# Four subtractions that move behind a normalisation in VectorE's queue

## The chip, the cores and the metric

The kernel runs on one core of a Trainium2 chip. The metric is the device time of one execution in microseconds. Before the change three runs gave 1221.09, 1221.14 and 1221.6 us; the median is 1221.14.

The engines are named as in the profile: PE is TensorE, PEld its weight loads, DVE is VectorE, ACT is ScalarE, POOL is GpSimd, SP is the engine that issues most transfers. L177 is line 177 of the kernel.

## The reference

The program computes two layers of a decoder trunk on 256 tokens of width 1024, in float32. Each layer is

```
x = LN(alpha*x + 0.5*SwiGLU_1(x))
x = LN(alpha*x + Mixer(x))
x = LN(alpha*x + 0.5*SwiGLU_2(x))

def _layernorm(x, g, b):
    mu = mean(x);  var = mean((x - mu)**2)
    return (x - mu) * rsqrt(var + 1e-5) * g + b

def _swiglu(x, w1, w3, w2):
    return (silu(x @ w1) * (x @ w3)) @ w2        # 1024 -> 2816 -> 1024
```

The mixer begins with one projection of x and holds a gated position mixing, a differential attention over 8 heads and an output projection. It matters here only in that its first product needs the normalised x, as the first product of a feed-forward block does.

## The kernel before, in words

**Products in three parts.** Every float32 operand is split into a high part (a copy of type fp32r, which the matmuls take) and a low part, what the copy lost. A product is the sum of three matmuls, high by high, high by low, low by high (`three`, L255). So each weight matrix that comes from memory takes three steps: a load of 1 MB into one of four buffers (`raw`), a copy by ScalarE into `whi` (L173), and a subtraction by VectorE that gives `wlo` (L177). The buffer is free for another load once both have read it. `stream` does this for one load. Its argument `after` names an instruction behind which the subtractions are put in VectorE's queue; an empty one means `latest[1]`, the last low part of the input's own split.

**Tokens and order.** The 256 tokens are two tiles of 128. TensorE's order is that of the program text, with side work put between the products by a list of tasks that count TensorE's progress (`beat`, `beside`). On the other engines a scheduler sets the order, bound by the data and by `behind(ins)`, which ties what is traced inside it behind `ins` on the same engine.

**The norm.** A feed-forward block ends with the class `Norm`. For each token tile, `finish_s` forms the mean, has ScalarE sum the squares (L536), computes the reciprocal root by a chain of small VectorE instructions (`rsqrt`, L227 to L233, 128x1 each), and normalises the rows in two halves of 512 columns (L539). The second of these two instructions is kept as `ends[t]`. Then each half is turned: four transposes by TensorE into a side bank (L608), gain and offset by ScalarE (L614), and a split into high (L217) and low (L218) part. `xlo[t, h]` keeps the low part's instruction of half h of tile t. The turned rows are what the next product reads; `self.x[0]` holds the first half's columns, `self.x[1]` the second's.

**The next product.** Behind a feed-forward norm the next matrix is multiplied by `gemm_b2`: for the first token tile, c = 0 and 1 (halves of the depth), m = 0 and 1 (halves of the width); then the same for the second tile. Four loads serve it. The first two are prepared inside the block before (`ahead`, `rest_of`; then `norm.pre` is set), the third and the fourth by `stream` at c = 1. The fourth load (n = 3, c = 1, m = 1) is the last stream that the change speaks of; `after[3]` is its tie. TensorE multiplies the first tile with the first three loads and turns the two halves of the second tile in between: the first half after six of the twelve matmuls of the third load, the second half after six of the twelve of the fourth.

There are three such places in a run: the first feed-forward norm of either layer (next is the mixer's value projection, `in_wb`) and the second feed-forward norm of the first layer (next is `in_w13b` of the second layer). Behind the mixer's norms `norm.pre` is not set.

Of the kernel before, what the change touches and what calls it, by code (L numbers as in the profile page):

```python
# [57 lines left out]
def trunk(ctx, tc, x, xT, w13a, w13b, w2s, w2p, wb, wqk, wa, wbr, wo, gateb, sgug, sgub, sguwT, sgubias, lam, diffg,  # L58
# [22 lines left out]
    def bank():  # L81
        return psum.tile([P, 512], F32, tag="main", name=name("bank"))
# [67 lines left out]
    def behind(ins):  # L150

        return tc.issue_after(ins) if ins is not None else nullcontext()

    def stream(src, width=CH, sub=HC, lent=(), after=(None, None)):

        step()
        raw = raw_pool.tile([P, CH], F32, tag="raw", name=name("raw"))
        nc.sync.dma_start(raw[:, :width], src)  # L160
        out = []
        for o in range(0, width, HC):
            if o // HC in lent:
                hi, lo = ([act.tile([P, 512], F32R, tag="slot", name=name(n)) for _ in range(2)] for n in ("lhi", "llo"))
                at = [(hi[j], lo[j]) for j in range(2)]
            else:
                hi = hi_pool.tile([P, HC], F32R, tag="hi", name=name("whi"))
                lo = lo_pool.tile([P, HC], F32R, tag="lo", name=name("wlo"))
                at = [(hi[:, p : p + sub], lo[:, p : p + sub]) for p in range(0, HC, sub)]
            for p, (h, w) in zip(range(0, HC, sub), at):  # L170
                r = raw[:, o + p : o + p + sub]
                with behind(latest[0] if o // HC in lent else early[0] or latest[0]):
                    copied = A.activation(h, r, AF.Copy)  # L173
                if o // HC in lent:
                    early[0] = copied.ins
                with behind(after[o // HC] or latest[1]):
                    V.tensor_tensor(out=w, in0=r, in1=h.bitcast(F32), op=ALU.subtract)  # L177
            out.append((hi, lo))
        return out
# [22 lines left out]
    def rest_of(pre, after):  # L202

        (_, hi0, lo0), (raw, hi1, lo1) = pre
        lows(pre[1], after)
        hi = hi_pool.tile([P, HC], F32R, tag="hi", name=name("whi"))
        lo = lo_pool.tile([P, HC], F32R, tag="lo", name=name("wlo"))
        for p in range(0, HC, 512):
            r, h, w = (v[:, o + p : o + p + 512] for v, o in ((raw, HC), (hi, 0), (lo, 0)))
            with behind(early[0]):  # L210
                A.activation(h, r, AF.Copy)
            with behind(after):
                V.tensor_tensor(out=w, in0=r, in1=h.bitcast(F32), op=ALU.subtract)
        return [(hi0[:2], lo0[:2]), (hi0[2:], lo0[2:])], [(hi1, lo1), (hi, lo)]
# [71 lines left out]
    def rows_b(ps, t, k0, piece, xh, xl, kts, c0=0, n=512):  # L286

        hi, lo = piece
        for j in range(2):
            k, o = k0 + j, j * 512 + c0  # L290
            wh, wl = (w[j][:, c0 : c0 + n] if isinstance(w, list) else w[:, o : o + n] for w in (hi, lo))
            three(ps[:, :n], xh(k)[:, t * P : (t + 1) * P], xl(k)[:, t * P : (t + 1) * P], wh, wl,
                  k == 0, k == kts - 1)
        beat(n / 1024)
# [66 lines left out]
    def gemm_b2(srcs, xh, xl, done, norm=None):  # L361

        lent, after = [()] * 4, [(None, None)] * 4
        if norm:
            lent = [(0, 1), (0,), (), ()]
            after[1:3] = [(norm.ends[0], norm.ends[0])] * 2
        ps = [[bank() for _ in range(2)] for _ in range(NT)]
        got = [[None] * 4 for _ in range(2)]  # L370
        for t in range(NT):
            for c in range(2):
                if norm:
                    norm.ready(t, c)
                    after[3] = [norm.xlo.get((0, 1))] * 2
                for m in range(2):
                    n = 2 * c + m
                    if t == 0 and n < 2 and norm and norm.pre:
                        if n == 0:
                            got[0][:2], got[1][:2] = rest_of(norm.pre, norm.ends[0])  # L380
                    elif t == 0:
                        got[m][2 * c : 2 * c + 2] = stream(srcs[m][:, c * CH : (c + 1) * CH], sub=512, lent=lent[n],
                                                           after=after[n])
                    for i in range(2 * c, 2 * c + 2):
                        rows_b(ps[t][m], t, 2 * i, got[m][i], xh, xl, KT)
            early[0] = None
            with behind(latest[0] if t == 0 else None):
                done(t, ps[t])
# [238 lines left out]
    def ffn(l, f, i, norm, following=None):  # L627
# [59 lines left out]
        if norm is None:  # L687
            gemm_first([w13b[l, f, 0, 0], w13b[l, f, 1, 0]], front(0))
        else:
            gemm_b2([w13b[l, f, 0, 0], w13b[l, f, 1, 0]], xh, xl, front(0), norm=norm)  # L690
# [65 lines left out]
    def mixer(l, i, norm):  # L756
# [6 lines left out]
        def got_val(t, ps):  # L763
            for h in range(2):
                A.activation(val[t][:, h], ps[h], AF.Copy)

        gemm_b2([wb[l, VAL_, 0], wb[l, VAL_, 1]], xh, xl, got_val, norm=norm)

        hb = slots("hb", 2 * KT, F32R)
# [200 lines left out]
        def done(t, ps):  # L970
            for h in range(2):
                ln.part(t, h * 512, ps[h])
            ln.finish(t, ((2, 1.5), (2, 1))[t])

        gemm_b2([wo[l, 0], wo[l, 1]], view(m_hi), view(m_lo), done)
        return ln.close()

    norm = None
    for l in range(DEPTH):
        norm = ffn(l, 0, 0, norm, [wb[l, 1, m] for m in range(2)])  # L980
        norm = mixer(l, 1, norm)
        norm = ffn(l, 1, 2, norm, [w13b[l + 1, 0, m, 0] for m in range(2)] if l < DEPTH - 1 else None)
# [92 lines left out]
```

## Time and profile before

| what | value |
|---|---|
| runs | 1221.09, 1221.14, 1221.6 us |
| profiled execution, its own time | 1220.97 us |
| its span | 1219.3 us |
| granted TensorE clock | 1.00 |
| PE busy | 1210.0 us (99%) |
| DVE busy | 948.8 us (78%) |
| ACT busy | 820.0 us (67%) |
| POOL busy | 87.7 us (7%) |
| L177, subtractions | 396 instructions, 437.8 us |
| L255 and its like, 128x512 matmul | 0.39 us each by the profile |
| read from memory | 235.47 MB |

Times inside the profile count from the start of the span. The matmuls are pipelined: each shows some 0.39 us, but the next starts 0.23 us after it. What TensorE loses is therefore read from start to start, and the idle time that the profile prints in brackets ahead of an instruction is somewhat less than the loss. A row of waits reads: engine and line that waited, what it waited for, microseconds in total, times, longest.

### The profile page before, as it was taken

How to read it: one execution, taken by the hardware profiler on the slowest of the kernel's cores; microseconds unless marked ns; L12 is line 12 of the kernel's file. 1: busy time of each engine (PE TensorE's matmuls, PEld its weight loads, DVE VectorE, ACT ScalarE, POOL GpSimd, SP SyncE). 2: the span in 40 equal slices, each digit the busy share in tenths (PEclk: the TensorE clock that was granted, in tenths of full speed). 3: DMA queues.
4: the chain of work that ended last, by engine and by line, in shares of the span. 5: the costliest groups of instructions: out<-in, count | busy, mean ns of one | idle time of the engine just before them, and what ended most of it. 6: DMA issues, size and time to landing. Idle time of an engine off the chain costs nothing.

```text
span 1219.3 us, 16603 instructions
## 1 busy us (share of the span) xinstructions
PE 1210.0 (99%) x6033; PEld 1018.2 (84%) x6033; DVE 948.8 (78%) x1540; ACT 820.0 (67%) x1340; POOL 87.7 (7%) x184
## 2 busy tenths in 40 slices
PE   9999999999999999999999999999999999999998
PEld 8888888888888888888878888888888888888886
DVE  6658998886587985579985679979856879747797
ACT  7677676689665575775766776666786655667761
POOL 0100000244100000000000000002430000000000
PEclk9999999999999999999999999999999999999999
DMA  8976666654644667665667655656546456576551
GB/s 319 334 246 178 218 226 214 214 169 165 249 171 167 216 176 264 192 202 210 218 218 252 194 176 205 255 215 202 165 175 232 173 172 243 177 238 209 181 202 48
DMA packets 82339, 252.29 MB, mean 207 GB/s; under 512 B 47520, under 2 KB 48592, under 8 KB 55632
## 3 DMA queue, kind: packets, MB, share of 16 engines
q1 hardware_dynamic: 78288, 238.31, 58.1%
q0 software_dynamic: 3536, 12.13, 3.1%
q8 instruction: 47, 0.77, 0.2%
q10 hardware_dynamic: 432, 0.79, 0.2%
q14 instruction: 36, 0.29, 0.1%
HBM read 235.47 MB, written 1.05 MB: 194 GB/s over the span
## 4 chain that ended last, share of the span: by engine, by line
PE 97%; DVE 1%; ACT 1%; DMA 0%; issue 0%; DVEq 0%; ACTq 0%
PE bank L255 36%; PE sbank L255 26%; PE bank L267 17%; PE bank L274 9%; PE sbank L267 2%; PE bank L430 2%; PE sbank L274 1%; PE sbank L805 1%; PE sbank L608 1%; DVE wlo L177 1%; PE sbank L854 1%; PE sbank L935 1%; ACT xf L614 0%; ACT sq L536 0%; PE sbank L852 0%; PE sbank L876 0%
## 5 line engine op out<-in xcount | busy, mean ns | idle before, releaser
L177 DVE TENSOR_TENSOR wlo<-raw,whi 128x1024 fp32r<-128x1024 f32 (+1 forms) x396 | 437.8, 1122 | 158.9 <-ACT whi L173 118.7
L173 ACT ACTIVATE whi<-raw 128x1024 fp32r<-128x1024 f32 (+1 forms) x396 | 375.5, 972 | 163.8 <-PE bank L255 61.7
L255 PE MATMUL bank<-whi,x 128*128 128x512 f32 x840 | 264.6, 390 | 0.0
L255 PEld LDWEIGHTS bank<-whi,x 128*128 128x128 f32 x840 | 157.7, 188 | 32.5
L255 PE MATMUL bank<-wlo,x 128*128 128x512 f32 x420 | 163.5, 389 | 0.0
L255 PE MATMUL sbank<-whi,x 128*128 128x512 f32 x512 | 159.0, 389 | 0.0
L267 PE MATMUL bank<-x,whi 128*128 128x512 f32 x640 | 158.3, 395 | 0.0
L267 PEld LDWEIGHTS bank<-x,whi 128*128 128x128 f32 x640 | 116.5, 188 | 25.9 <-issue 2.6
L255 PEld LDWEIGHTS sbank<-whi,x 128*128 128x128 f32 x512 | 96.1, 188 | 20.0
L337 ACT ACTIVATE shi<-raw 128x1024 fp32r<-128x1024 f32 (+1 forms) x80 | 73.4, 946 | 51.7 <-DVE raw L352 26.4
L255 PE MATMUL sbank<-wlo,x 128*128 128x512 f32 x256 | 99.6, 389 | 0.0
L339 DVE TENSOR_TENSOR slo<-raw,shi 128x1024 fp32r<-128x1024 f32 (+1 forms) x80 | 85.3, 1088 | 14.1 <-ACT shi L337 13.1
L255 PEld LDWEIGHTS bank<-wlo,x 128*128 128x128 f32 x420 | 78.9, 188 | 16.0
L274 PE MATMUL bank<-x,wlo 128*128 128x256 f32 x640 | 85.9, 285 | 0.0
L274 PEld LDWEIGHTS bank<-x,wlo 128*128 128x128 f32 x640 | 81.6, 191 | 2.3
L275 ACT ACTIVATE r<-bank 128x256 f32<-128x256 f32 x112 | 41.9, 379 | 27.6 <-PE bank L274 27.6
L614 ACT ACTIVATE xf<-sbank,ln_b,ln_g 128x128 f32<-128x128 f32 x80 | 30.0, 455 | 42.1 <-PE sbank L608 42.1
L255 PE MATMUL sbank<-whi,hhi 128*128 128x512 f32 x144 | 56.4, 391 | 0.0
L255 PEld LDWEIGHTS sbank<-wlo,x 128*128 128x128 f32 x256 | 48.0, 188 | 9.9
L255 PE MATMUL sbank<-wlo,hhi 128*128 128x512 f32 x144 | 56.1, 389 | 0.0
L255 PE MATMUL sbank<-whi,hlo 128*128 128x512 f32 x144 | 56.1, 389 | 0.0
L490 POOL DMA_DIRECT2D bc<-in_lng x6 | 3.2, 532 | 711.2 <-DVE bc L489 711.2
(246 smaller groups left out, 1984.6 us busy)
## 6 DMA issues: line engine op xcount, KB each, us to landing
raw<-in_w13b SPq DMA_DIRECT2D x76, 1024.0 KB, 5.3
raw<-in_w2p SPq DMA_DIRECT2D x24, 1024.0 KB, 4.8
raw<-in_wa SPq DMA_DIRECT2D x24, 1024.0 KB, 5.3
raw<-in_w2s SPq DMA_DIRECT2D x20, 1024.0 KB, 4.8
raw<-in_wb SPq DMA_DIRECT2D x16, 1024.0 KB, 5.2
raw<-in_wqk SPq DMA_DIRECT2D x16, 1024.0 KB, 5.0
raw<-in_wbr SPq DMA_DIRECT2D x16, 1024.0 KB, 4.8
raw<-in_w13a SPq DMA_DIRECT2D x8, 1024.0 KB, 4.8
```

Source lines behind the costliest of these rows:

```text
L173: copied = A.activation(h, r, AF.Copy)
L177: V.tensor_tensor(out=w, in0=r, in1=h.bitcast(F32), op=ALU.subtract)
L255: PE.matmul(ps, xx, w, start=start and n == 0, stop=stop and n == 2)
L267: PE.matmul(b[-1], hi[:, k * P : (k + 1) * P], xc(k), start=k == 0, stop=False)
L274: PE.matmul(b[n][:, :T], lo[:, k * P : (k + 1) * P], xc(k)[:, :T], start=False, stop=k == KT - 1)
L275: emptied[0] = A.activation(r[:, s], b[n][:, T:], AF.Copy, scale=scale).ins
L337: A.activation(h, r, AF.Copy)
L339: V.tensor_tensor(out=w, in0=r, in1=h.bitcast(F32), op=ALU.subtract)
L430: PE.matmul(ps[t][m], x[:, j, o + t * P : o + (t + 1) * P], y, start=k0 + j == 0 and o == 0 and y is hi, stop=k0 + j == KT - 1 and y is lo)
L608: PE.transpose(b[:, k * P : (k + 1) * P], self.y[t][:, h * 512 + k * P : h * 512 + (k + 1) * P], ident)
L614: A.activation(xf[:, s], b[:, s], AF.Identity, scale=self.gT[:, f], bias=self.bT[:, f])
L805: PE.matmul(banks[m][:, j * nk : (j + 1) * nk], rows(qT, m, j, t * P, P), rows(kT, m, j, 0, nk), start=True, stop=True)
```

## The change

One line of `gemm_b2` is changed. Where the input comes from a feed-forward norm, the fourth load's subtractions are tied behind `norm.ends[1]`, the second half of the second token tile's normalisation, instead of behind the low part of the first tile's second half. Behind a mixer norm the tie stays as it was.

```diff
             for c in range(2):
                 if norm:
                     norm.ready(t, c)
-                    after[3] = [norm.xlo.get((0, 1))] * 2
+                    after[3] = [norm.ends[1] if norm.pre else norm.xlo.get((0, 1))] * 2
                 for m in range(2):
```

No instruction is added or removed, and the order on PE, ACT, POOL and SP stays as it was. VectorE's order differs at the three places. The first of them, at the end of the first layer's first feed-forward block (xtok_144 is the second token tile, nwy and nwa are the links of its reciprocal root, wlo_1817 and wlo_1823 the low parts of the fourth load, x_1207 and x_1208 the turned rows); - is before, + is the change:

```order
 L218 TENSOR_TENSOR x_1208<-xf_1707,x_1208 128x4x128
 L233 TENSOR_SCALAR nwy_1725<-nwa_1724,yi_1721 128x1
-L177 TENSOR_TENSOR wlo_1817<-raw_1814,whi_1816 128x512
 L232 TENSOR_SCALAR nwa_1728<-nwy_1725,ve_1720 128x1
-L177 TENSOR_TENSOR wlo_1817<-raw_1814,whi_1816 128x512
 L233 TENSOR_SCALAR nwy_1729<-nwa_1728,nwy_1725 128x1
-L177 TENSOR_TENSOR wlo_1823<-raw_1814,whi_1822 128x512
 L232 TENSOR_SCALAR nwa_1732<-nwy_1729,ve_1720 128x1
-L177 TENSOR_TENSOR wlo_1823<-raw_1814,whi_1822 128x512
 L233 TENSOR_SCALAR nwy_1733<-nwa_1732,nwy_1729 128x1
 L539 TENSOR_SCALAR xtok_144<-xtok_144,mv_1715,nwy_1733 128x512 x2
+L177 TENSOR_TENSOR wlo_1817<-raw_1814,whi_1816 128x512 x2
+L177 TENSOR_TENSOR wlo_1823<-raw_1814,whi_1822 128x512 x2
```

The four subtractions stood one by one between the links of the root; now they stand together behind the two halves of the normalisation, ahead of the low parts of the second tile's turned rows (L218).

TensorE's order at the same place, which is the same before and after, shows who reads them. whi_1784 and wlo_1785 belong to the third load, sbank_1796 and sbank_1834 take the turned halves of the second tile:

```order
L608 MATMUL sbank_1796<-ident,xtok_144 128x128 [waits DMASW1_49,DVE_49]
L608 MATMUL sbank_1796<-ident,xtok_144 128x128 x3
L255 MATMUL bank_1740<-whi_1784,x_1208 128x512
L255 MATMUL bank_1740<-wlo_1785,x_1208 128x512
L255 MATMUL bank_1740<-whi_1784,x_1208 128x512 x2
L255 MATMUL bank_1740<-wlo_1785,x_1208 128x512
L255 MATMUL bank_1740<-whi_1784,x_1208 128x512
L255 MATMUL bank_1741<-whi_1816,x_1208 128x512
L255 MATMUL bank_1741<-wlo_1817,x_1208 128x512 [waits DVE_49]
L255 MATMUL bank_1741<-whi_1816,x_1208 128x512 x2
L255 MATMUL bank_1741<-wlo_1817,x_1208 128x512 [waits DVE_49]
L255 MATMUL bank_1741<-whi_1816,x_1208 128x512
```

These are the rows after the change. The rows stand where they stood; new are the waits for VectorE at the two matmuls that read wlo_1817, and in the same way at the two that read wlo_1823 behind the next transposes.

## The prediction

> **What bounds the kernel now.** First the head of the page, with the busy time of the engines and the shares of the chain of waits that ended last:
>
> ```profile
> span 1219.3 us, 16603 instructions
> PE 1210.0 (99%) x6033; PEld 1018.2 (84%) x6033; DVE 948.8 (78%) x1540; ACT 820.0 (67%) x1340; POOL 87.7 (7%) x184
> PE 97%; DVE 1%; ACT 1%; DMA 0%; issue 0%; DVEq 0%; ACTq 0%
> ```
>
> TensorE is busy 99% of the span and carries 97% of the chain. Nothing can be gained on another engine unless TensorE stands still for it. So the second view is the list of TensorE's waits; these four rows are all of it, and the row of the weight loads that belongs to the first stands below them:
>
> ```profile
> PE sbank L608 <- DVE xtok L539: 2.9, 3, 1.0
> PE sbank L442 <- DVE warm L438: 1.0, 1, 1.0
> PE sbank L576 <- DVE xtok L555: 1.0, 1, 1.0
> PE sbank L580 <- ACT minus L578: 0.2, 1, 0.2
> PEld sbank L608 <- DVE xtok L539: 4.2, 3, 1.4
> ```
>
> The transposes of the normalised rows (L608) wait three times for L539, the normalisation itself: 2.9 us by TensorE's row and 4.2 us by that of the weight loads. The others lie at the start and at the end of the program. The third view is TensorE's timeline around those three waits, and around a group of the same transposes that did not wait (177.64):
>
> ```profile
> 177.41 0.39 PE L255 MATMUL sbank<-whi,hlo 128*128 128x512 f32 x1
> 177.64 0.60 PE L608 MATMUL sbank<-ident,xtok 128*128 128x128 f32 x4
> 178.00 0.48 PE L255 MATMUL sbank<-whi,hhi 128*128 128x512 f32 x1
> ...
> 189.28 0.39 PE L255 MATMUL bank<-whi,x 128*128 128x512 f32 x1
> 190.65 0.66 PE L608 MATMUL sbank<-ident,xtok 128*128 128x128 f32 x4 [0.98 <-DVE xtok L539]
> 191.06 0.48 PE L255 MATMUL bank<-whi,x 128*128 128x512 f32 x1
> ...
> 614.05 0.39 PE L255 MATMUL bank<-whi,x 128*128 128x512 f32 x1
> 615.41 0.65 PE L608 MATMUL sbank<-ident,xtok 128*128 128x128 f32 x4 [0.97 <-DVE xtok L539]
> 615.82 0.48 PE L255 MATMUL bank<-whi,x 128*128 128x512 f32 x1
> ...
> 793.57 0.39 PE L255 MATMUL bank<-whi,x 128*128 128x512 f32 x1
> 794.93 0.66 PE L608 MATMUL sbank<-ident,xtok 128*128 128x128 f32 x4 [0.97 <-DVE xtok L539]
> 795.34 0.48 PE L255 MATMUL bank<-whi,x 128*128 128x512 f32 x1
> ```
>
> The durations overlap, so a stall is read from starts. Unhindered, the matmul after the transposes starts 178.00 - 177.41 = 0.59 us behind the matmul ahead of them. In the three waits it is 191.06 - 189.28 = 1.78, 615.82 - 614.05 = 1.77 and 795.34 - 793.57 = 1.77. The stalls are therefore 1.19, 1.18 and 1.18 us, together 3.55. Without a stall the transposes would start 0.23 us behind the matmul ahead of them (177.64 - 177.41), that is at 189.51 instead of 190.65.
>
> **What the change removes.** At each of the three places VectorE runs the rsqrt chain of the second token tile (L232 and L233 in turn on 128x1), then L539 in two halves. Four subtractions (L177, 128x512) stand between the chain's links. These are VectorE's rows at the first place, and then the same links for the first token tile, where nothing stands between them:
>
> ```profile
> 186.79 0.21 DVE L233 TENSOR_SCALAR nwy<-nwa,yi 128x1 f32<-128x1 f32 x1
> 186.91 0.68 DVE L177 TENSOR_TENSOR wlo<-raw,whi 128x512 fp32r<-128x512 f32 x1
> ...
> 189.20 0.68 DVE L177 TENSOR_TENSOR wlo<-raw,whi 128x512 fp32r<-128x512 f32 x1
> 189.80 0.21 DVE L233 TENSOR_SCALAR nwy<-nwa,nwy 128x1 f32<-128x1 f32 x1
> 190.04 1.00 DVE L539 TENSOR_SCALAR xtok<-xtok,mv,nwy 128x512 f32<-128x512 f32 x2
> ...
> 173.98 0.21 DVE L233 TENSOR_SCALAR nwy<-nwa,yi 128x1 f32<-128x1 f32 x1
> 175.35 1.01 DVE L539 TENSOR_SCALAR xtok<-xtok,mv,nwy 128x512 f32<-128x512 f32 x2
> 176.27 0.68 DVE L524 SCALAR_TENSOR_TENSOR xtok<-xtok,sbank 128x512 f32<-128x512 f32 x1
> 176.87 0.69 DVE L524 SCALAR_TENSOR_TENSOR xtok<-xtok,v 128x512 f32<-128x512 f32 x1
> ```
>
> From the first L233 to L539 it is 190.04 - 186.79 = 3.25 us with the subtractions, and 175.35 - 173.98 = 1.37 us without. The price of the bare chain is thus bounded by 1.37 and 3.25. I take 1.37: it is the same links on the same engine, 13 us earlier. The first L233 stays at 186.79, since all that stands ahead of it keeps its place. L539 then starts at 186.79 + 1.37 = 188.16 instead of 190.04. TensorE began 190.65 - 190.04 = 0.61 us after L539's start, which is the first half and the signal, so the transposes can run from 188.77. TensorE comes to them at 189.51. The data are 0.74 us early and the whole stall goes. The reserve also says how good the price must be: up to a chain of 1.37 + 0.74 = 2.11 us nothing of the gain is lost; beyond that each 0.1 us costs 0.1 us at each place. That the other two places are the same shows in VectorE's busy time (second number, with its instructions) from that first L233 to the end of L539's first half:
>
> ```profile
> 186.79:190.59 3.80, 3.76 (x12) 1.00 0.67 261
> 611.55:615.35 3.80, 3.76 (x12) 1.00 0.69 263
> 791.07:794.87 3.80, 3.76 (x12) 1.00 0.68 261
> ```
>
> **What it moves, and what is late next.** The four subtractions now stand behind L539. Behind L539 the next instruction starts 0.92 us after L539's start (176.27 - 175.35), and 128x512 instructions follow each other by 0.60 (176.87 - 176.27). So they start at 189.08, 189.68, 190.28 and 190.88 and end, 0.69 each, at 189.77 up to 191.57. Three things wait on them or behind them.
>
> First TensorE's matmuls, which today read the first and the last of the four at
>
> ```profile
> 192.74 0.39 PE L255 MATMUL bank<-wlo,x 128*128 128x512 f32 x1
> 195.25 0.39 PE L255 MATMUL bank<-wlo,x 128*128 128x512 f32 x1
> ```
>
> and, 1.19 earlier, at 191.55 and 194.06. The first subtraction is 1.78 us ahead of its reader, the last 2.49. Each of the two halves between them has as much within a few tenths. These matmuls get a wait of their own, which the wait for L539 covered until now; it is met long before, so I price it at nothing.
>
> Second, on VectorE's queue behind them, the low part of the second tile's turned rows (L218), which waits for ScalarE, and ScalarE for the transposes:
>
> ```profile
> 193.54 0.69 DVE L218 TENSOR_TENSOR x<-xf,x 128x512 fp32r<-128x512 f32 x1 [2.50 <-ACT x L217]
> 204.58 2.00 ACT L173 ACTIVATE whi<-raw 128x1024 fp32r<-128x1024 f32 x2
> ```
>
> Moved by 1.19 it can start at 192.35, and VectorE is free at 191.57. The 2.50 us of idle time ahead of it are the cover; without it, each tenth of a microsecond over would push L218, and no more. So the entire sequence of transposes, L614, L217 and L218 moves forward with TensorE.
>
> Third the input buffer. The last of the four subtractions is what frees it, and the queue of loads waits for that:
>
> ```profile
> 189.94 0.33 SPq L160 DMA_DIRECT2D raw<-in_wqk x1
> 203.12 2.60 SPq L160 DMA_DIRECT2D raw<-in_wqk  x2
> ...
> raw<-in_wqk SPq DMA_DIRECT2D x1, 1024.0 KB, 4.8
> ```
>
> Today the subtraction ends at 189.20 + 0.68 = 189.88 and the load goes out at 189.94. It will go out at about 191.57 + 0.06 = 191.63, 1.69 us later, and land at 196.43 instead of 194.74. Its data are the fourth 1 MB piece of the next stage; the ScalarE row above begins with the second half of the third piece, and the fourth follows as the second of that row's two at some 205.5, or 204.3 after the shift. That is a reserve of 7.9 us, and the next load goes out only at 203.12, when the next stage has freed a buffer. No instruction is added or taken away, so VectorE, ScalarE and the queues do the same work.
>
> **Sum.** The profiled execution took 1220.97 us, span 1219.3 plus 1.67 around it. 1220.97 - 1.19 - 1.18 - 1.18 = 1217.42. The median of the runs, 1221.14, lies 0.17 above the profiled execution (runs from 1221.09 to 1221.6), which gives 1217.59 from there; I say 1217.5. The size of the stall itself has bounds: 2.9 us by TensorE's idle time (which the overlapping durations make too small), 4.2 us by that of the weight loads, hence 1218.1 and 1216.8.
>
> **Rivals.**
>
> *The chain stays slow.* The bare chain takes more than 2.11 us, for instance because its links cost more while ScalarE reads the same rows. Halfway from 2.11 to today's 3.25 it keeps 0.57 us of the 1.14 us by which the transposes are late: about 1.7 of the 3.55 us are left, 1219.2. Against it: the links of the first tile took 1.37 with the same neighbours. Chance 0.05.
>
> *The gap is a shortage of buffers, or the gain is taken back further on.* The transposes would wait for a free side bank rather than for L539, or a later wait on something that does not shift would take up the 1.19; the time stays at 1221.0. The bank that the second tile's first transposes take was last read by VectorE in this row:
>
> ```profile
> 178.67 0.69 DVE L528 SCALAR_TENSOR_TENSOR xtok<-xtok,sbank 128x512 f32<-128x512 f32 x1
> ```
>
> It was free at 179.4, ten microseconds before it is wanted, and the four rows of TensorE's waits show no wait behind these places that could take something up. Chance 0.07. [...]
>
> *Slower.* The later release of the input buffer decides. If the fourth piece of the next stage set its pace, that stage would begin 1.69 us later than today at each place, the gain ahead of it would be lost, and the time would be 1220.97 + 3 x 1.69 = 1226.0. That begins where the load takes more than 4.8 + 7.9 = 12.7 us. For it speaks that the release is really put off; against it the 4.8 us of the load and the reserve. Chance 0.03.
>
> **How the numbers follow.** The forecast, all three stalls gone, has 0.85, and its own range is 1216.8 to 1218.3, from the bounds of the stall and the scatter of the runs. The range reaches to the slow chain's 1219.2; what it leaves out, no change, slower and the worse half of the slow chain, is about 0.13. A measurement of this kernel can tell about 0.2% from no change, that is 2.4 us, or 1218.7. Faster than that: the forecast and somewhat less than half of the slow chain, 0.87. Within 0.2%: 0.07 and the rest of the slow chain, 0.10. Slower: 0.03.
>
> **What would show it.** The changed kernel's list of TensorE's waits has no row L608 <- L539, and PEld's neither; the matmul behind the transposes starts 0.59 us after the one ahead of them at all three places; L539 follows the first L233 of its chain by about 1.4 us; four L177 follow it without a gap; L218 still waits for ScalarE. A row that has TensorE wait for wlo L177 would show the moved work late, one that has ScalarE wait for a load in the stage behind would show the buffer. The forecast is wrong if L539 comes more than 2.1 us behind that L233, or if the stall is gone and the span is not shorter by about 3.5.

## The result and the profile after

The changed kernel takes 1217.84 us (median of eight runs, 1217.45 to 1218.23); the kernel before, on the same chip, takes 1221.2 (eight runs, 1221.03 to 1221.96). That is 3.36 us less, a ratio of 0.9971 with a 95% interval of 0.996 to 0.9982 (0.29% less, 0.18% to 0.4%). The forecast was 1217.5, its range 1216.8 to 1219.2. The profiled execution took 1217.86 us, 3.11 less than the one before.

The head of the changed kernel's page, with the busy times and the shares of the chain of waits:

```profile
span 1216.2 us, 16603 instructions
PE 1209.8 (99%) x6033; PEld 1018.9 (84%) x6033; DVE 949.7 (78%) x1540; ACT 820.0 (67%) x1340; POOL 87.8 (7%) x184
PE 99%; DMA 0%; DVE 0%; ACT 0%; DVEq 0%; issue 0%; ACTq 0%
```

The busy times are those of before within 1 us. TensorE's share of the chain rose from 97% to 99%, and VectorE's went from 1% to 0. The list of TensorE's waits, all of it:

```profile
PE sbank L442 <- DVE warm L438: 1.0, 1, 1.0
PE sbank L576 <- DVE xtok L555: 1.0, 1, 1.0
PE sbank L580 <- ACT minus L578: 0.2, 1, 0.2
```

The row L608 <- L539 is gone, and no row has taken its place. TensorE's timeline at the three places (start, duration, instruction):

```profile
189.41 0.39 PE L255 MATMUL bank<-whi,x 128*128 128x512 f32 x1
189.64 0.60 PE L608 MATMUL sbank<-ident,xtok 128*128 128x128 f32 x4
189.99 0.49 PE L255 MATMUL bank<-whi,x 128*128 128x512 f32 x1
...
613.02 0.39 PE L255 MATMUL bank<-whi,x 128*128 128x512 f32 x1
613.26 0.60 PE L608 MATMUL sbank<-ident,xtok 128*128 128x128 f32 x4
613.61 0.48 PE L255 MATMUL bank<-whi,x 128*128 128x512 f32 x1
...
791.36 0.39 PE L255 MATMUL bank<-whi,x 128*128 128x512 f32 x1
791.59 0.60 PE L608 MATMUL sbank<-ident,xtok 128*128 128x128 f32 x4
791.94 0.49 PE L255 MATMUL bank<-whi,x 128*128 128x512 f32 x1
```

From the matmul ahead of the transposes to the one behind them it is now 0.58, 0.59 and 0.58 us, where it was 1.78, 1.77 and 1.77: 3.57 us less in all. VectorE at the first place:

```profile
186.91 0.21 DVE L233 TENSOR_SCALAR nwy<-nwa,yi 128x1 f32<-128x1 f32 x1
...
188.02 0.21 DVE L233 TENSOR_SCALAR nwy<-nwa,nwy 128x1 f32<-128x1 f32 x1
188.27 1.00 DVE L539 TENSOR_SCALAR xtok<-xtok,mv,nwy 128x512 f32<-128x512 f32 x2
189.19 2.49 DVE L177 TENSOR_TENSOR wlo<-raw,whi 128x512 fp32r<-128x512 f32 x4
192.48 0.69 DVE L218 TENSOR_TENSOR x<-xf,x 128x512 fp32r<-128x512 f32 x1 [0.80 <-ACT x L217]
```

The chain from the first L233 to L539 takes 188.27 - 186.91 = 1.36 us. This execution runs 0.13 us late from its first 8 us on, so the rows at this place stand 0.10 to 0.13 later than forecast. The four subtractions end at 189.19 + 2.49 = 191.68. Their first and last readers, then the load that waits for the last of them, and the ScalarE rows of the next stage:

```profile
191.70 0.40 PE L255 MATMUL bank<-wlo,x 128*128 128x512 f32 x1
...
194.24 0.39 PE L255 MATMUL bank<-wlo,x 128*128 128x512 f32 x1
```

```profile
191.75 0.33 SPq L160 DMA_DIRECT2D raw<-in_wqk  x1
...
203.56 2.00 ACT L173 ACTIVATE whi<-raw 128x1024 fp32r<-128x1024 f32 x2
```

The load goes out at 191.75 (forecast 191.63), and the ScalarE row, whose second instruction reads it from 204.51 on, has no idle time ahead of it. The moved work is late for nobody.

**Where a part of the gain went.** Laid side by side matmul by matmul, TensorE starts 0.13 us late and gains 3.50 us on the kernel before at the three places, so that it is 3.36 us ahead behind the third. It keeps this until 874 us. Then it loses 0.3 us in one group of the attention's score matmuls (L805), here in the kernel after and then in the kernel before:

```profile
874.85 1.42 PE L805 MATMUL sbank<-qk,qk 64*128 64x256 f32 x8
```

```profile
878.22 1.13 PE L805 MATMUL sbank<-qk,qk 64*128 64x256 f32 x8
```

The loss comes from 24 us earlier. VectorE scales probabilities (L832, L824) while GpSimd forms a product of the rotary embedding (L781). First VectorE's and GpSimd's timelines of the kernel after, then of the kernel before:

```profile
850.57 0.22 DVE L832 SCALAR_TENSOR_TENSOR c<-rc,neg_lam,sums 128x4 f32<-128x4 f32 x1
850.83 2.43 DVE L824 SCALAR_TENSOR_TENSOR pp<-pp,c,pp 128x256 f32<-128x256 f32 x4
850.96 1.49 POOL L781 TENSOR_TENSOR swap<-swap,sin_t 128x512 f32<-128x512 f32 x1 [4.78 <-DVE c L832]
```

```profile
853.92 0.96 DVE L832 SCALAR_TENSOR_TENSOR c<-rc,neg_lam,sums 128x4 f32<-128x4 f32 x1
854.92 1.41 DVE L824 SCALAR_TENSOR_TENSOR pp<-pp,c,pp 128x256 f32<-128x256 f32 x4
853.58 1.28 POOL L781 TENSOR_TENSOR swap<-swap,sin_t 128x512 f32<-128x512 f32 x1 [4.04 <-DMA swap<-z]
```

Before, L832 is held until about the end of L781 (it ends at 854.88, L781 at 854.86) and takes 0.96 us instead of 0.22. After, L781 begins a little later against VectorE, 0.39 us behind the start of L832 instead of 0.34 ahead of it, and one of the four L824 is held instead: it takes 1.50 us from 851.23 on, the one ahead of it 0.48. From the start of L832 to the end of the last L824 it is 2.41 us before and 2.69 after. Behind them VectorE's work is 3.07 us ahead of before, where it had been 3.36 ahead, and ten microseconds later ScalarE's is 3.08 ahead. TensorE, still 3.36 ahead, loses the difference when it reaches this L805; 0.26 of it remains to the end. So the profile's gain is 3.50 - 0.13 (start) - 0.26 = 3.11, and the spans differ by 3.1.

### The profile page after: what moved, and what is told of

It is laid out like the page before. It is cut to its first block, busy times and chain, and to the rows that moved or that the text cites. A ratio compares the mean times of both kernels' runs of the same rounds, so it can differ in the third digit from the quotient of the medians.

```text
span 1216.2 us, 16603 instructions
## 1 busy us (share of the span) xinstructions
PE 1209.8 (99%) x6033; PEld 1018.9 (84%) x6033; DVE 949.7 (78%) x1540; ACT 820.0 (67%) x1340; POOL 87.8 (7%) x184
## 3 DMA queue, kind: packets, MB, share of 16 engines
HBM read 235.47 MB, written 1.05 MB: 194 GB/s over the span
## 4 chain that ended last, share of the span: by engine, by line
PE 99%; DMA 0%; DVE 0%; ACT 0%; DVEq 0%; issue 0%; ACTq 0%
PE bank L255 38%; PE sbank L255 26%; PE bank L267 17%; PE bank L274 9%; PE sbank L267 2%; PE bank L430 2%; PE sbank L274 1%; PE sbank L805 1%; PE sbank L608 1%; PE sbank L854 1%; PE sbank L935 1%; PE sbank L852 0%; PE sbank L876 0%; PE sbank L839 0%; DMA xraw<-in_xT 0%; PE sbank L844 0%
## 5 line engine op out<-in xcount | busy, mean ns | idle before, releaser
L614 ACT ACTIVATE xf<-sbank,ln_b,ln_g 128x128 f32<-128x128 f32 x80 | 30.1, 457 | 38.6 <-PE sbank L608 38.6
```

Of the source, the lines that this page charges most:

```text
L614: A.activation(xf[:, s], b[:, s], AF.Identity, scale=self.gT[:, f], bias=self.bT[:, f])
```

## The experiments

**One place alone.** If the three stalls are independent and each is the order on VectorE, the tie at the first place alone takes a third of the gain, and nothing elsewhere.

```diff
-    after[3] = [norm.xlo.get((0, 1))] * 2
+    after[3] = [norm.ends[1] if norm.pre and norm.first else norm.xlo.get((0, 1))] * 2
...
-    self.ends, self.xlo, self.pre = [None] * NT, {}, None
+    self.ends, self.xlo, self.pre, self.first = [None] * NT, {}, None, (l, i) == (0, 0)
```

> The new tie at the first of the three places only (the first layer's first feed-forward norm); the other two as before. If the late normalisation alone makes the stall, the places are independent: TensorE has lost 1.1 to 1.2 us at the first place less than before and waits for L539 at the other two, 0.97 us of idle time each; about 1220.0 us. If a shortage of banks or buffers sets the gap, the first place keeps its gap and the time stays at 1221.2.

Measured: 1220.08 us (1219.8 to 1220.91; before 1221.25), ratio 0.9991, interval 0.9981 to 1.0. TensorE's list of waits has, of the row in question,

```profile
PE sbank L608 <- DVE xtok L539: 1.9, 2, 1.0
```

Two waits are left of three. Against the changed kernel TensorE falls back by 1.12 and 1.13 us at the other two places, and by less than 0.1 anywhere else. The places are independent, and a third of the change takes a third of the gain. A shortage of buffers or banks would not have yielded to the order at one place.

**Half the subtractions moved.** This puts the chain's length between the two known ones, near the break-even of 2.11 us. The tie holds only for the second of the load's two half-width pieces.

```diff
-    after[3] = [norm.xlo.get((0, 1))] * 2
+    after[3] = [norm.xlo.get((0, 1)), norm.ends[1] if norm.pre else norm.xlo.get((0, 1))]
```

> At all three places only two of the four subtractions stand behind the normalisation, the other two stay between the links of the chain. By the rows of the changed kernel the distance from the first L233 to L539 is then 1.36 plus twice some 0.47, about 2.3 us, so the transposes can start 0.2 us later than TensorE comes to them: 3 x 0.2 = 0.6 us of the gain is lost, about 1218.4 us. If each subtraction in the chain cost the same quarter of the stall, half the gain would be lost and the time would be 1219.5.

Measured: 1218.46 us (1218.24 to 1219.09), ratio 0.9977, interval 0.9968 to 0.9986. VectorE and TensorE at the first place:

```profile
186.93 0.21 DVE L233 TENSOR_SCALAR nwy<-nwa,yi 128x1 f32<-128x1 f32 x1
...
189.23 1.00 DVE L539 TENSOR_SCALAR xtok<-xtok,mv,nwy 128x512 f32<-128x512 f32 x2
```

```profile
189.42 0.39 PE L255 MATMUL bank<-whi,x 128*128 128x512 f32 x1
189.84 0.66 PE L608 MATMUL sbank<-ident,xtok 128*128 128x128 f32 x4
190.25 0.48 PE L255 MATMUL bank<-whi,x 128*128 128x512 f32 x1
```

The chain is 189.23 - 186.93 = 2.30 us long, and the stall 190.25 - 189.42 - 0.58 = 0.25. At the other two places it is 0.23 and 0.24. A chain 0.19 over the break-even costs some 0.2 at each place, as the rule of the reserve says. TensorE's row prints no idle time here, because the durations overlap: the stall shows only from start to start.

**More links in the chain.** The changed kernel with two or six further dependent multiplications by 1.0 (128x1) ahead of the second tile's L539. They cost VectorE time but move nothing else. The diff is that of six; with two, the last line has 2 * t.

```diff
+    def again(y, n):
+        for _ in range(n): z, x = sm('nwy', 1), y; V.tensor_scalar(out=z, in0=x, scalar1=1.0, scalar2=None, op0=ALU.mult); y = z
+        return y
...
-    def rsqrt(v, eps, scale=1.0):
+    def rsqrt(v, eps, scale=1.0, more=0):
...
-        return y
+        return again(y, more)
...
-            r = rsqrt(ss, self.eps, 1.0 / D)
+            r = rsqrt(ss, self.eps, 1.0 / D, 6 * t)
```

> The changed kernel with six more links of the chain, multiplications by 1.0 on 128x1, behind the root of the second token tile at the three places. At 0.19 to 0.25 us a link the chain grows by 1.1 to 1.5 us, of which the reserve of 0.76 us swallows the first part: TensorE waits 0.4 to 0.8 us for L539 at each place, 1219.0 to 1220.1 us. Without a reserve, every link lost would show: 1221.1 to 1222.3. If the chain is not what the transposes wait for, 1217.8.

> The changed kernel with two more links of the chain at the three places. Six cost 1.2 us of the gain, 0.19 us of chain each beyond the reserve of 0.76 us. Two are 0.38 us and lie within the reserve: TensorE's starts at the three places are those of the changed kernel, 1217.8 us. Without a reserve it would be 3 x 0.38 = 1.1 us longer, 1218.9.

Measured: six links 1219.05 us (1218.69 to 1219.62), ratio 0.9981, interval 0.9972 to 0.9991; two links 1217.99 (1217.72 to 1218.6), ratio 0.9973, interval 0.9962 to 0.9984. With six links, at the first place:

```profile
188.92 1.09 DVE L220 TENSOR_SCALAR nwy<-nwy 128x1 f32<-128x1 f32 x6
190.05 1.00 DVE L539 TENSOR_SCALAR xtok<-xtok,mv,nwy 128x512 f32<-128x512 f32 x2
```

```profile
190.06 0.39 PE L255 MATMUL bank<-whi,x 128*128 128x512 f32 x1
190.65 0.66 PE L608 MATMUL sbank<-ident,xtok 128*128 128x128 f32 x4 [0.21 <-DVE xtok L539]
191.06 0.48 PE L255 MATMUL bank<-whi,x 128*128 128x512 f32 x1
```

Six links delay L539 by 190.05 - 188.92 = 1.13 us, but TensorE loses only 191.06 - 190.06 - 0.58 = 0.42 (0.36 to 0.41 when the starts are compared with the changed kernel's). The difference of some 0.75 is the reserve; the forecast had 0.74. Two links, 0.38 us, cost nothing: TensorE's starts at this place are those of the changed kernel. The six links' 1.21 us over the changed kernel is 3 x 0.4.

**The subtractions moved too far.** Now the fourth load's subtractions stand behind the low part of the second tile's first half (L218), which itself waits for the transposes, L614 and L217. TensorE needs them by then, so the price of a tie that is too late shows; the input buffer is released late with it.

```diff
     for m in range(2):
-        n = 2 * c + m
+        n = 2 * c + m; after[3] = [norm.xlo[1, 0]] * 2 if t == 0 and n == 3 and norm and norm.pre else after[3]
```

> The four subtractions are tied still later, behind the low part of the second tile's first turned half (L218). The first ends then at about 193.8 us where TensorE wants it at 191.7: a wait of TensorE for wlo L177 of 2.1 us at each of the three places, none for L539, 1224.1 us, slower than before. The input buffer is also freed some 4 us later than in the changed kernel. If the late buffer mattered, ScalarE would wait for a load in the stage behind and the loss would be more than 2.1 us a place; if not, the wait for wlo is all of it.

Measured: 1227.06 us (1226.41 to 1227.59), ratio 1.0048, interval 1.0031 to 1.0064. It is slower, and by 3 us more than expected. TensorE waits three times for the subtractions:

```profile
PE bank L255 <- DVE wlo L177: 5.9, 3, 2.0
```

From start to start the three gaps are equal (2.35, 2.36, 2.35 us), but behind the first of them the loss goes on. The view by stretches, with PE's busy time and instructions, the other engines', then the granted clock as the third number from the end: the gap at the first place, the ten matmuls behind it, the same ten at the second place, and the whole stretch at a lower clock at the first.

```profile
192.10:194.45 2.35, 0.40 (x3) 0.01 (x1) 1.35 (x3) 0.93 (x2) 0.00 (x0) 1.00 0.00 0
194.45:197.39 2.94, 2.94 (x10) 2.37 (x10) 1.75 (x3) 0.00 (x0) 0.00 (x0) 0.52 0.09 11
621.91:623.53 1.62, 1.62 (x10) 1.35 (x10) 1.62 (x3) 0.00 (x0) 0.00 (x0) 1.00 0.00 0
194.59:198.00 3.41, 3.41 (x11) 2.75 (x12) 1.61 (x3) 0.27 (x1) 0.00 (x0) 0.50 0.16 34
```

At the first place the clock is granted at 0.52 over the ten, and they take 2.94 us instead of 1.62; it stands at 0.50 for 3.41 us. Until it recovers TensorE loses 3.8 us there against the changed kernel, and 2.2 at each of the other two, 8.2 in all: 6.5 from the gaps and 1.7 from the clock. The profiled execution, at 1226.59 us, is 8.73 longer than the changed kernel's; 0.6 of that was lost in its first 8 us, and has to do with none of the places. The four runs lie between 1226.41 and 1227.59 and only one has a trace, so what the clock cost the others, and with it the rest of the median, stays open. The buffer was released 4.5 us later than in the changed kernel:

```profile
196.26 0.33 SPq L160 DMA_DIRECT2D raw<-in_wqk  x1
...
207.99 2.00 ACT L173 ACTIVATE whi<-raw 128x1024 fp32r<-128x1024 f32 x2
```

ScalarE comes to the next stage's pieces without waiting for a load. But its row stands 207.99 - 203.56 = 4.43 us later too, since TensorE's loss moves the whole stage. From the load's landing (4.7 to 4.8 us after it goes out) to the copy that reads it, it is 7.9 us here, 8.1 in the changed kernel and 10.8 before. So this run tests no later release than the change's own, which is without a price.

**TensorE turned later instead.** The kernel before, with VectorE's order at the three places untouched (in the attention six of its instructions stand elsewhere), but TensorE turns the second tile's first half six matmuls later: the numbers that `finish_s` gets for this tile, its waits counted in loads of twelve matmuls, are 2.5 and 0.5 in place of 2 and 1. If the stall is nothing but data that come too late, asking later removes it as well.

```diff
-            (ln.finish if last else ln.finish_s)(t, ((2, 1.5), (2, 1))[t])
+            (ln.finish if last else ln.finish_s)(t, ((2, 1.5), (2.5, 0.5))[t])
```

> The kernel before, with VectorE's order as it was, but TensorE turns the second tile's first half six matmuls (1.36 us) later, behind all twelve of the third load. The normalisation is as late as before; TensorE comes to it at 190.87 where the data are ready at 190.65. If the stall is only that TensorE comes too early to late data, it is gone as in the changed kernel: no wait for L539, 1217.8 us. If what matters is that the whole sequence of turning is early, the second tile's matmuls wait for the turned rows instead and part of the gain is lost.

Measured: 1217.06 us (1216.76 to 1217.53; before 1221.21), ratio 0.9966, interval 0.9953 to 0.9978. TensorE at the first place:

```profile
190.49 0.40 PE L255 MATMUL bank<-whi,x 128*128 128x512 f32 x1
190.72 0.60 PE L608 MATMUL sbank<-ident,xtok 128*128 128x128 f32 x4
191.08 0.48 PE L255 MATMUL bank<-whi,x 128*128 128x512 f32 x1
```

VectorE's chain is as slow as before (L233 at 186.64, L539 at 189.90: 3.26 us), and the stall is gone all the same. So what counts is only that L539 comes before TensorE asks; the change's way is one of two. The median lies 0.8 us below the changed kernel's, the profiled execution 1.1. Side by side the profiles show 0.05 of this at each place and 0.27 at L805 (0.78 from the first to the last start of the group, against 1.05). Another 0.28 is there before the first place is reached, and the profiles scatter more than that: the first L233 of that place, ahead of which nothing was changed, starts at 186.64 here, at 186.91 in the changed kernel and at 187.56 with six links. The remaining 0.4 lies behind the last matmul: from its start to the end of the span it is 4.04 us, in the changed kernel 4.45 and before 4.46. What shortens it stays open.

**The tie at every norm.** The mixer's norms had kept the old tie.

```diff
-    after[3] = [norm.xlo.get((0, 1))] * 2
+    after[3] = [norm.ends[1]] * 2
```

> The changed kernel with the tie also behind the two mixer norms. There the transposes start 0.33 us behind the matmul ahead of them instead of 0.23. The wait goes: 2 x 0.1 = 0.2 us less, 1217.6 us, not to be told from the changed kernel by time, but to be seen in TensorE's starts. If the subtractions come late there, TensorE waits for wlo and the time is longer than 1217.8.

Measured: 1217.47 us (1217.24 to 1218.18), ratio 0.997, interval 0.9959 to 0.9982. TensorE gains 0.14 and 0.13 us at the two mixer norms, and in this profile nothing is lost at L805. By the times it can't be told from the changed kernel.

**The rest of the gap at L805.** The changed kernel was profiled twice more, and once with the rotary product L781 on VectorE instead of GpSimd.

```diff
-            turned_by[0] = G.tensor_tensor(out=s3, in0=s3, in1=s, op=ALU.mult).ins
+            V.tensor_tensor(out=s3, in0=s3, in1=s, op=ALU.mult)
```

> The changed kernel once more, one look. The three stalls are gone again. In the first profile 0.3 us of the 3.5 us was given back in the second layer's attention, where a GpSimd instruction (L781) and VectorE's L824 ran at the same moment. If that is chance of the transfer that GpSimd waits for, the 0.3 us is at another place or absent and the span is between 1215.7 and 1216.5; if the change causes it, it is there again at the same matmuls (L805).

> The changed kernel again, on the chip of these runs: 1217.5 to 1218.2 us, for the comparison with the kernels beside it. TensorE loses 0 to 0.3 us at the fourth group of L805 in the second layer, as the GpSimd instruction falls.

> The changed kernel with the rotary product L781 moved from GpSimd to VectorE, so that no GpSimd instruction of that size runs beside VectorE in the attention. If L832 (0.22 or 0.96 us) and the four L824 (1.4 or 2.4 us together) were long because of L781 on GpSimd, they are 0.22 and 1.4 us everywhere now. VectorE gets 16 instructions of about 0.7 us more and another order, so the time itself says nothing here, perhaps 1217 to 1225 us. If their length has another cause, the long ones remain.

Measured: 1218.14 us for the repetition in a single run, 1217.74 (1217.5 to 1218.45) in six runs; 1217.75 in a single run with L781 on VectorE. From the first to the last start of the L805 group it is 0.76 us before, 1.05 in the first profile after, 0.91 and 0.98 in the repetitions, and 0.76 with L781 on VectorE. How long L832 and L824 take in the whole program (the view of one line: least, median, most in ns), first in the kernel after and then with L781 on VectorE:

```profile
L832 DVE SCALAR_TENSOR_TENSOR c<-rc,neg_lam,sums x8: 215/223/1241, 235.4 to 884.6; 128x4 f32<-128x4 f32 x8
L824 DVE SCALAR_TENSOR_TENSOR pp<-pp,c,pp x32: 335/410/1501, 235.9 to 886.2; 128x256 f32<-128x256 f32 x16, 128x128 f32<-128x128 f32 x16
```

```profile
L832 DVE SCALAR_TENSOR_TENSOR c<-rc,neg_lam,sums x8: 214/216/223, 234.5 to 884.0; 128x4 f32<-128x4 f32 x8
L824 DVE SCALAR_TENSOR_TENSOR pp<-pp,c,pp x32: 343/410/481, 235.3 to 885.5; 128x256 f32<-128x256 f32 x16, 128x128 f32<-128x128 f32 x16
```

Without a GpSimd product beside them no L832 takes over 0.23 us and no L824 over 0.48, and the loss at L805 is gone from the trace. So the hold goes with L781, as the held instruction's end near L781's end shows too: the longest L832 of the kernel after (1.24 us, from 866.95 on) ends at 868.19, its L781 at 868.17.

That the loss at L805 follows from the hold is shown less well, since this move also changes the order on VectorE and ScalarE in the attention. For it speaks that the two agree wherever VectorE's order there is kept: VectorE falls back against the kernel before at the hold by 0.29 us in the first profile after, by 0.17 and 0.25 in the repetitions and by 0.04 with the tie at every norm, and the group of L805 loses 0.29, 0.15, 0.22 and nothing. So the loss is no fixed price of the change; it varies with where L781 falls. The hold alone isn't enough for a loss: with the later turn, L781 is on GpSimd, L832 takes 1.22 us and VectorE falls back by 0.26 as well, but in its other order it has caught up when TensorE comes to L805.

**Both combined.** The later turn at the feed-forward norms, the tie at the mixer norms alone; then the same with L781 on VectorE.

```diff
-    after[3] = [norm.xlo.get((0, 1))] * 2
+    after[3] = [norm.xlo.get((0, 1)) if norm.pre else norm.ends[1]] * 2
...
-            (ln.finish if last else ln.finish_s)(t, ((2, 1.5), (2, 1))[t])
+            (ln.finish if last else ln.finish_s)(t, ((2, 1.5), (2.5, 0.5))[t])
```

> The kernel before with TensorE's later turning at the feed-forward norms (as in the run that turned later) and the new tie at the two mixer norms only. The two gains lie at different places and add up: no wait for L539, and the transposes behind the mixer norms 0.1 us earlier each, 1217.06 - 0.2 = about 1216.9 us, below the changed kernel. If the place of the turning is paid for elsewhere, it is not below 1217.8.

> The same with the rotary product L781 on VectorE instead of GpSimd, which took away the long L832 and L824. It should be no slower, 1216.6 to 1217.0 us; the gain is at most the 0.3 us that TensorE lost at L805 in some profiles. If VectorE's 16 further instructions come late somewhere, it is slower than 1217.0.

Measured: 1216.86 us (1216.7 to 1217.32), ratio 0.9964, interval 0.9952 to 0.9977; with L781 on VectorE 1216.78 (1216.64 to 1217.28), ratio 0.9963, interval 0.995 to 0.9975. These are the lowest medians of the study, some 1 us below the changed kernel's, whose six runs on the same chip begin at 1217.5; 0.08 between the two is no difference, so L781 may stay on GpSimd. The 1 us is not all gained at the norms. The first kernel's profile gains about 0.4 us on the changed kernel's there, 0.27 at L805 and 0.4 behind the last matmul, as with the later turn alone.

## Why the prediction was right

- **The stall from starts (3.55 us): right.** TensorE's starts gave 3.57 at the three places (3.50 somewhat behind them). Both rows of waits would have misled: 2.9 us by TensorE's, 4.2 by the weight loads'. The run with one place confirms 1.1 to 1.2 per place.
- **The bare chain (1.37 us): right**, 1.36 at all three places. The price came from the same links at the first token tile in the same profile.
- **The reserve (0.74 us): right**, about 0.75 by the six links, not used up by the two.
- **What is late next: right, nothing.** The first subtraction starts at 189.19 and ends, after its 0.69 us, 1.82 ahead of its reader at 191.70 (forecast 1.78), the last 194.24 - 191.68 = 2.56 ahead of its own (forecast 2.49). L218 waits for ScalarE as before, now 0.80 us. The load left 0.12 later than forecast and was not missed: it lands 8.1 us ahead of the copy that reads it (forecast 7.9). No run cuts that lead by more than another 0.2 us; where the release came 4.5 us later, the stage came 4.4 us later as well.
- **The sum: 0.3 us too good.** 1220.97 - 3.55 = 1217.42 was made for the profiled execution, which took 1217.86. The step that failed is the sentence on the rival that "a later wait on something that does not shift would take up the 1.19", which was ruled out since "the four rows of TensorE's waits show no wait behind these places that could take something up". The list shows waits that exist, not such as arise: at L805 the profile after lost 0.29, 0.26 of it for good, behind a GpSimd product that held VectorE longer than in the profile before. What sets that product's place against VectorE is not settled: its row names a transfer before and VectorE's L832 after. Together with the late start of 0.13 and 3.50 in place of 3.55 this is the difference of 0.44. By the medians, 3.36 against 3.55, less is missing; a part of the 0.3 may be scatter between executions, since the eight runs lie 0.78 us apart (1217.45 to 1218.23).
- **The rivals.** *Slow chain*: no, 1.36; the half-moved kernel shows what a chain just over the break-even would have cost. *Shortage of buffers*: no, by the run with one place, where the order alone took the first of the three waits away and left the other two. *Taken back further on*: true in kind and small, a twelfth in the first profile and less in the repetitions. *Late release*: no, with 8.1 us to spare.

## What to carry to other kernels

The independent work between the links of a chain of small dependent instructions was good here for the engine's throughput and bad for the chain's latency. The eleven instructions from the first L233 on end after 4.25 us with the subtractions between the links (186.79 to 191.04) and after 4.77 with them behind (186.91 to 191.68); L539 begins after 3.25 and after 1.36 us. Where another engine stands waiting for the chain's end, put the work behind it, or let the waiting engine ask later, and measure first by how much the result may be late (a few dummy links do it). Read a stall from start to start against an unhindered group, and don't take a list of today's waits as proof that a gain isn't taken back.

## What the runs showed of the hardware

**The clock after a short gap.** Where the subtractions came too late, a gap of 2.35 us from start to start was followed at the first of the three places by a granted clock of 0.50 for 3.41 us, a further loss of about 1.7 us. At the second place the same gap left the clock at 1.00 (621.91 to 623.53). At the third TensorE lost no more than at the second, 2.2 us, and the mean clock of the whole execution, 0.999, has room for one such stretch only: 3.41 us at 0.50 take 0.0014 from it, two would take 0.0028. The kernel before, with 1.78, 1.77 and 1.77 us from start to start at the same three places, has a clock of 1.00 there (188 to 194, 612.5 to 618.5, 792 to 798). What decides among the three was not tried.

**VectorE held by GpSimd.** Where L781 runs on GpSimd, VectorE's scalar_tensor_tensor took up to 1.24 us in L832 and up to 1.50 us in L824; with L781 on VectorE it took 0.22 and 0.48 at most. In the kernel before, the held L832 ends at 854.88 us and L781 at 854.86. In the kernel after, the longest L832 ends at 868.19 and its L781 at 868.17, and the held L824 at 851.23 + 1.50 = 852.73, 0.28 behind L781 (850.96 + 1.49 = 852.45). What holds VectorE there no run shows beyond that, and whether other instructions are held the same way was not tried.
